# Encoder layer with a 32-expert mixture: TensorE's order by hand from the third expert on, and four bias matmuls at another place

## The chip, the core and the metric

The kernel runs on one core of a Trainium2 chip. The metric is the device time of one execution in microseconds (us). The core's engines run their own instruction lists in order: TensorE (PE; its weight loads are listed apart as PEld), VectorE (DVE), ScalarE (ACT), GpSimd (POOL) and SyncE (SP, which here issues the loads of weights). They wait for each other by semaphores.

## What is computed

One post-norm layer on 1024 tokens of width 1024: attention, a LayerNorm, and then a mixture of experts, in which each token goes to 4 of 32 experts. The part that the change touches is the mixture; cut to it, the reference is:

```python
def clamped_swiglu(h):
    h_glu = jnp.minimum(h[..., 0::2], SWIGLU_LIMIT)
    h_lin = jnp.clip(h[..., 1::2], -SWIGLU_LIMIT, SWIGLU_LIMIT)
    return h_glu * jax.nn.sigmoid(SWIGLU_ALPHA * h_glu) * (h_lin + 1.0)

def expert_block(args):                       # 128 rows of one expert
    xblk, e = args
    h = xblk @ w_gate_up[e] + b_gate_up[e]    # 1024 -> 2048
    return clamped_swiglu(h) @ w_down[e] + b_down[e]   # 1024 -> 1024
```

The result of each block is scaled by the rows' gates and added to the tokens' rows.

## The kernel before

**Experts.** Each expert takes 128 rows; the 18 experts with most tokens (numbers 1 to 6 and then the even ones from 8 to 30; `ovf(e)` is true for them) take 32 rows more, "rows beyond 128". The loop over experts is unrolled, and runs `gate_up(e)` and then `down(e - 1)`, so that an expert's activation is transposed and multiplied by its down weights one expert later.

**Blocks.** `gate_up(e)` runs over 8 blocks k of 128 weight rows (tiles w3g and so on: expert 3, gate and up), `down(e)` over 4 blocks of 256 (w3d). Products of float32 are made in three passes: the weights are split into a rounded part `wh`, by a cast on ACT (L615), and the rest `wl`, by a subtraction on DVE (L620), and the rows into `xTh`, `xTl` (for down: `aTh`, `aTl`). A block is 12 matmuls of 128x512. `wh` and `wl` have three buffers each, so the cast for block k + 3 waits until TensorE has done block k. The matmuls of gate_up add up in PSUM tiles gu_0 and gu_1, those of down in yp, those of the rows beyond 128 in go and yq (groups of 16 matmuls of 32 columns, after the blocks 3 and 7, and at the end of down).

**Biases.** They are matmuls of a one-hot row, `sel`, with the table of biases (tile b3, in the trace b): four into gu at the head of an expert (gu<-b,sel), and four of 32 columns into go (go<-b,sel) for the rows beyond 128.

**Transposes.** The rows reach TensorE transposed. `turn` transposes four pieces of 128x128 into the PSUM tile tp and splits the result: a cast on ACT (L60, `xTh`/`aTh`), then a subtraction on DVE (L61, `xTl`/`aTl`), which is the last reader of tp. **There is one buffer for tp**, so a transposition waits until the one before it has been read out:

```python
            tc.tile_pool(name="moet", bufs=1, space=PSUM, reuse_waits="tile") as ps_t:
...
def turn(src, hi, lo, nk, nm):
    tp = ps_t.tile([P, 4, P], F32, tag="tp", name=f"tp{nm}")
    for c in range(nk):
        nc.tensor.transpose(tp[:, c, :], src[:, c * P:(c + 1) * P], ident)
    ...
        split(hi, lo, tp[:, 0:nk, :])
```

Per expert e these are, in the order in which the code asks for them: tpa_0, tpa_1 and (if expert e - 1 has rows beyond 128) tpao of the activation of e - 1, behind the blocks 0, 1 and 2; and tpx_0, tpx_1 and (if expert e + 1 has such rows) tpxo of the rows of e + 1, behind the blocks 3, 4 and 5 (for e = 2 behind 4, 5 and 6).

**What sets the order.** A scheduler orders each engine's list at compile time by its own estimates of when an instruction can start, and may put a transposition or a bias between two matmuls of a block. Inside `tc.manual_schedule(engines={PE})` TensorE's list keeps the order in which the code is written. Before, this holds for `down` of the experts with rows beyond 128 alone. ACT and DVE are ordered by the scheduler throughout the experts.

Of the kernel before, what the change touches and what calls it, by code (L numbers as in the profile page):

```python
# [20 lines left out]
P = 128  # L21
# [9 lines left out]
OVF = 32  # L31
# [11 lines left out]
def trunk_kernel(ctx: ExitStack, tc: tile.TileContext, x, w_qkv, q_norm, k_norm, w_o,  # L43
# [7 lines left out]
    def mm(o, lhsT, rhs, start=True, stop=True):  # L51
        nc.tensor.matmul(o, lhsT=lhsT, rhs=rhs, start=start, stop=stop)  # L52
# [525 lines left out]
    b3 = keep.tile([P, 2 * D], BF16, name="b3")  # L578
# [4 lines left out]
    sel = keep.tile([P, NE], BF16, name="sel")  # L583
# [461 lines left out]
    with tc.tile_pool(name="moex", bufs=1, side="right", reuse_waits="tile") as mx, \  # L1045
# [83 lines left out]
        def ovf(e):  # L1129
            rank = e if e < 2 else e // 2 + (NE // 2 if e % 2 else 1)  # L1130
            return 1 <= rank <= NO
# [78 lines left out]
        def gate_up(e, between):  # L1210
            gus = [ps_g.tile([P, D], F32, tag=f"gu{h}", name=f"gu{e}_{h}") for h in range(2)]
            gu = [gus[n // 2][:, n % 2 * 512:(n % 2 + 1) * 512] for n in range(4)]
            if ovf(e):
                go = ps_o.tile([P, 512], F32, tag="o", name=f"go{e}")
            for n in range(4):
                sl = slice(n * 512, (n + 1) * 512)
                mm(gu[n], sel[:, e:e + 1].to_broadcast([P, P]), b3[:, sl], True, False)
            for n in range(4 if ovf(e) else 0):
                mm(go[n * OVF:(n + 1) * OVF], sel[:, e:e + 1].to_broadcast([P, OVF]),
                   b3[:, n * 512:(n + 1) * 512], True, False)  # L1220
            act[e], part, whole = swiglu(gus, D, e)
            by_cols = e in (0, NE - 1)
            later = []
            for k in range(KD - 2 if by_cols else KD):
                fetch(ci[0] + len(order))
                prep(ci[0] + 3)
                hi, lo, w = wts.pop((e, "g", k))
                xh, xl = xT[e][0][:, k, :], xT[e][1][:, k, :]
                for n in range(4):
                    sl = slice(n * 512, (n + 1) * 512)  # L1230
                    mm3(gu[n], xh, xl, hi[:, sl], lo[:, sl], False, k == KD - 1)
                later.append((k, w))
                if k % 4 == 4 - 1:
                    for kk, w in later if ovf(e) else ():
                        j, hf = divmod(kk, 2)
                        ts = slice(j * OVF, (j + 1) * OVF)
                        for n in range(4):
                            mm(go[n * OVF:(n + 1) * OVF], xoT[e][:, hf, ts], w[:, n * 512:(n + 1) * 512],
                               False, kk == KD - 1)
                    later.clear()  # L1240
                ci[0] += 1
                if k in between:
                    between[k]()
            if by_cols:

                end = []
                for k in range(KD - 2, KD):
                    fetch(ci[0] + len(order))
                    prep(ci[0] + 3)
                    end.append((k, wts.pop((e, "g", k))))  # L1250
                    ci[0] += 1
                for n in range(4):
                    sl = slice(n * 512, (n + 1) * 512)
                    for k, (hi, lo, w) in end:
                        mm3(gu[n], xT[e][0][:, k, :], xT[e][1][:, k, :], hi[:, sl], lo[:, sl], False, k == KD - 1)
                    if n == 0:
                        for k in (KD - 2, KD - 1):
                            if k in between:
                                between[k]()
                    if n == 1:  # L1260
                        part(0)
                part(1)
            else:
                whole()
            xT.pop(e)
            if ovf(e):
                xoT.pop(e)
                acto[e], _, whole = swiglu([go], 256, f"o{e}")
                whole()

        def down(e, between={}):
            y = ys.pop(e, None) or mp.tile([P, D], F32, tag="y", bufs=2, name=f"y{e}")
            yp = ps_g.tile([P, D], F32, tag="gu0", name=f"yp{e}") if e == NE - 1 else \
                ps_y.tile([P, D], F32, tag="y", name=f"yp{e}")
            if ovf(e):
                yq = ps_o.tile([P, 512], F32, tag="o", name=f"yq{e}")
            ah, al = actT[e]
            later = []
            in_turn = ExitStack()
            if ovf(e):  # L1280
                in_turn.enter_context(tc.manual_schedule(engines={mybir.EngineType.PE}))
            for c in range(KD // 2):
                fetch(ci[0] + len(order))
                prep(ci[0] + 3)
                hi, lo, w = wts.pop((e, "d", c))
                for j in range(2):
                    k = 2 * c + j
                    for n in range(2):
                        sl = slice(j * D + n * 512, j * D + (n + 1) * 512)
                        mm3(yp[:, n * 512:(n + 1) * 512], ah[:, k, :], al[:, k, :], hi[:, sl], lo[:, sl],  # L1290
                            k == 0, k == KD - 1)
                later.append((c, w))
                if c == KD // 2 - 1:
                    for cc, w in later if ovf(e) else ():
                        ts = slice(cc * OVF, (cc + 1) * OVF)
                        for j in range(2):
                            for n in range(2):
                                sl = slice(j * D + n * 512, j * D + (n + 1) * 512)
                                m = 2 * j + n
                                mm(yq[m * OVF:(m + 1) * OVF], actoT[e][:, j, ts], w[:, sl],  # L1300
                                   cc == 0, cc == KD // 2 - 1)
                    later.clear()
                ci[0] += 1
                if c in between:
                    between[c]()
            in_turn.close()
            nc.scalar.mul(y, yp, gm_s[:, e:e + 1])  # L1307
            nc.gpsimd.indirect_dma_start(  # L1308
                out=fd, out_offset=bass.IndirectOffsetOnAxis(ap=mi[:, e:e + 1], axis=0),
                in_=y, in_offset=None, bounds_check=T + P - 1, oob_is_err=True, compute_op=ALU.add)  # L1310
            if not ovf(e):
                return
            H2 = 2 * OVF
            ya = mp.tile([H2, 512], F32, tag="ya", bufs=1, name=f"ya{e}")
            nc.scalar.mul(ya, yq[H2:P], go_s[H2:P, e:e + 1])
            yo = mp.tile([H2, 512], F32, tag="yo", bufs=2, name=f"yo{e}")
            nc.vector.scalar_tensor_tensor(yo, yq[0:H2], go_s[0:H2, e:e + 1], ya, ALU.mult, ALU.add)
            nc.gpsimd.indirect_dma_start(
                out=fd2, out_offset=bass.IndirectOffsetOnAxis(ap=toh[:, e:e + 1], axis=0),
                in_=yo, in_offset=None, bounds_check=2 * (T + P) - 1, oob_is_err=True, compute_op=ALU.add)  # L1320

        fetch(8)
        for e in range(NE):
            between = {}
            if e > 0:
                for part in range(3):
                    between[part] = lambda part=part: turn_a(e - 1, part)
            if e + 1 < NE:
                if e == 0:
                    between[X1] = lambda: [turn_x(1, part) for part in range(3)]  # L1330
                else:
                    for part in range(3):
                        between[(4 if e == 2 else 3) + part] = lambda part=part: turn_x(e + 1, part)
            if e == 0:
                with tc.manual_schedule(engines={mybir.EngineType.DVE}):
                    slots(lambda: prep_lo(2))
            gate_up(e, between)
            if e == 1:
                list_blocks()
            if e + 2 < NE:  # L1340
                gather_x(e + 2)
                gather_o(e + 2)
            if e == NE - 1:
                between = {1 + part: lambda part=part: turn_a(NE - 1, part) for part in range(3)}
                down(e - 1, between)
            elif e > 0:
                down(e - 1)
        down(NE - 1)

    es_w.close()  # L1350

# [141 lines left out]
```

## Time and profile before

| | |
|---|---|
| time, median of 3 runs | 2091.97 us (2090.58 to 2093.69) |
| the profiled execution: own time, span | 2091.31 us, 2089.5 us |
| TensorE (PE) busy | 1999.2 us, 96% of the span |
| DVE, ACT busy | 1636.2 us (78%), 1284.1 us (61%) |
| mean granted TensorE clock | 0.984 of full speed |

The span is the time from the first to the last instruction; 1.8 us of the execution lie around it. Busy is the sum of the durations of an engine's instructions. Matmuls are pipelined and their records overlap, so TensorE's pace is read from the starts of neighbouring rows, and not from their durations. The clock is given as a share of 2.4 GHz: 1.00 is full speed, 0.50 the level of 1.2 GHz.

### The profile page before, as it was taken

Reading aid. Unit: us, or ns where it says so; the run is one execution under the profiler, and the core shown is the slowest. Engines: PE = TensorE matmul, PEld = TensorE weight load, DVE = VectorE, ACT = ScalarE, POOL = GpSimd, SP = SyncE. Lnnn points to the kernel's source line nnn. Section 1 sums busy time; section 2 is a strip of 40 time slices with the busy share of each in tenths; the row PEclk is TensorE's granted clock in tenths of the full one; section 3 lists DMA queues with packets and bytes.
Section 4 is the critical chain, followed back from the end, with each engine's and each line's share of the span. In section 5 each row is a group of like instructions: output and inputs, shape, how many; then the busy total and the mean of one; then the engine's idle time right before and its main releaser. Section 6 shows DMA issues by size and latency. Waiting matters only on the chain. (4 is left out here: it accounts for less than half of the span.)

```text
span 2089.5 us, 27609 instructions
## 1 busy us (share of the span) xinstructions
PE 1999.2 (96%) x10059; PEld 1358.2 (65%) x10091; DVE 1636.2 (78%) x1771; ACT 1284.1 (61%) x1548; POOL 555.2 (27%) x382
## 2 busy tenths in 40 slices
PE   8999999999997999999999999999999999999990
PEld 6774444444675666666776776777767767777670
DVE  5658778887887877777887887878878878788786
ACT  5656655565554656656676766766767667667662
POOL 0216676766134311110210102111111021110114
PEclk9999999999998999999999999999999999999995
DMA  5216000000545778788897897898978978989764
GB/s 173 71 61 177 31 31 21 31 21 11 205 148 205 278 283 301 272 302 287 328 376 293 333 349 294 346 343 307 377 290 334 349 297 345 339 302 379 267 248 174
DMA packets 106348, 500.36 MB, mean 239 GB/s; under 512 B 16001, under 2 KB 17026, under 8 KB 73442
## 3 DMA queue, kind: packets, MB, share of 16 engines
q1 hardware_dynamic: 86928, 445.45, 55.3%
q0 software_dynamic: 16432, 52.47, 9.1%
q8 instruction: 80, 1.31, 0.3%
q10 hardware_dynamic: 2850, 0.66, 0.1%
q14 instruction: 58, 0.48, 0.1%
HBM read 457.05 MB, written 41.49 MB: 239 GB/s over the span
## 5 line engine op out<-in xcount | busy, mean ns | idle before, releaser
L52 PE MATMUL gu<-wh,xTh 128*128 128x512 f32 x1024 | 415.3, 406 | 1.0 <-ACT xTh L60 1.0
L52 PE MATMUL gu<-wh,xTl 128*128 128x512 f32 x1024 | 410.5, 401 | 0.0
L52 PE MATMUL gu<-wl,xTh 128*128 128x512 f32 x1024 | 401.9, 393 | 0.0
L1308 POOL DMA_INDIRECT fd<-y,mi x32 | 78.8, 2464 | 660.5 <-ACT y L1307 656.8
L447 ACT ACTIVATE pt<-st 128x512 f32<-128x512 f32 x256 | 150.6, 597 | 134.8 <-PE st L52 110.1
L52 PEld LDWEIGHTS gu<-wh,xTh 128*128 128x128 f32 x1024 | 193.4, 189 | 42.3 <-ACT xTh L60 1.7
L52 PEld LDWEIGHTS gu<-wh,xTl 128*128 128x128 f32 x1024 | 193.9, 189 | 38.5 <-issue 3.6
L52 PEld LDWEIGHTS gu<-wl,xTh 128*128 128x128 f32 x1024 | 193.3, 189 | 39.4 <-issue 0.2
L451 POOL TENSOR_TENSOR acc<-acc,pt 128x512 f32<-128x512 f32 x152 | 201.2, 1324 | 48.8 <-ACT pt L447 39.8
L52 PE MATMUL yp<-wl,aTh 128*128 128x512 f32 x512 | 204.5, 399 | 0.4 <-DVE wl L620 0.4
L52 PE MATMUL yp<-wh,aTh 128*128 128x512 f32 x512 | 201.8, 394 | 0.0
L52 PE MATMUL yp<-wh,aTl 128*128 128x512 f32 x512 | 200.0, 391 | 0.0
L437 DVE TENSOR_REDUCE nm<-sc 128x1 f32<-128x1024 f32 x124 | 150.5, 1221 | 29.1 <-PE sc L52 28.1
L52 PE MATMUL po<-pt,vn 128*64 128x512 f32 x512 | 135.7, 616 | 2.1 <-DVE ot L472 2.1
L606 POOL DMA_INDIRECT xg<-xd,mi x32 | 54.6, 1706 | 291.6 <-PE tpx L1145 282.5
L52 PE MATMUL qkv<-wh,xT 128*128 128x512 f32 x384 | 124.2, 404 | 2.6 <-ACT xT L60 1.4
L52 PE MATMUL st<-qs,kT_hi 128*128 128x512 f32 x256 | 116.7, 456 | 3.4 <-ACT pt L447 3.2
L52 PEld LDWEIGHTS yp<-wh,aTh 128*128 128x128 f32 x512 | 96.2, 188 | 33.5 <-ACT act L1189 14.2
L52 PEld LDWEIGHTS st<-qs,kT_hi 128*128 128x128 f32 x256 | 48.0, 188 | 97.7 <-ACT pt L447 66.7
L52 PEld LDWEIGHTS yp<-wl,aTh 128*128 128x128 f32 x512 | 96.4, 188 | 21.8 <-DVE wl L620 1.2
L52 PEld LDWEIGHTS yp<-wh,aTl 128*128 128x128 f32 x512 | 96.2, 188 | 20.2 <-issue 0.8
L52 PE MATMUL st<-q,kT_lo 128*128 128x512 f32 x256 | 102.4, 400 | 0.6 <-DVE q L155 0.6
(515 smaller groups left out, 4179.4 us busy)
## 6 DMA issues: line engine op xcount, KB each, us to landing
w0g<-in_expert_w_gate_up SPq DMA_DIRECT2D x8, 1024.0 KB, 19.6
w1g<-in_expert_w_gate_up SPq DMA_DIRECT2D x8, 1024.0 KB, 7.8
w2g<-in_expert_w_gate_up SPq DMA_DIRECT2D x8, 1024.0 KB, 10.4
w3g<-in_expert_w_gate_up SPq DMA_DIRECT2D x8, 1024.0 KB, 8.5
w4g<-in_expert_w_gate_up SPq DMA_DIRECT2D x8, 1024.0 KB, 6.4
w5g<-in_expert_w_gate_up SPq DMA_DIRECT2D x8, 1024.0 KB, 6.4
w6g<-in_expert_w_gate_up SPq DMA_DIRECT2D x8, 1024.0 KB, 6.5
w7g<-in_expert_w_gate_up SPq DMA_DIRECT2D x8, 1024.0 KB, 7.1
```

Source lines behind the costliest of these rows:

```text
L52: nc.tensor.matmul(o, lhsT=lhsT, rhs=rhs, start=start, stop=stop)
L437: nc.vector.tensor_reduce(nms[n][:, m:m + 1], sc.pop((n, m)), AX.X, ALU.max, negate=True)
L447: nc.scalar.activation(pts[n, k], st, AF.Exp)
L451: (nc.vector if k == 7 or n == NG - 1 or n == NG - 2 and k > 3 else nc.gpsimd).tensor_tensor(accs[n], pts[n, 0] if k == 1 else accs[n], pt ...
L606: return nc.gpsimd.indirect_dma_start(out=xg[e], out_offset=None, in_=xd, in_offset=bass.IndirectOffsetOnAxis(ap=mi[:, e:e + 1] if rows is ...
L1308: nc.gpsimd.indirect_dma_start(out=fd, out_offset=bass.IndirectOffsetOnAxis(ap=mi[:, e:e + 1], axis=0), in_=y, in_offset=None, bounds_chec ...
```

## The change

The context for TensorE's own order is opened once, after `gate_up(1)` and `list_blocks()`, and closed after the last `down`, in place of one context for each `down` of an expert with rows beyond 128. So from expert 2 (the third) on TensorE's list is the order of the code. In `gate_up`, the four bias matmuls into go move from the head of the expert to just ahead of the first group of matmuls into go, behind block 3.

```diff
@@ gate_up
             for n in range(4):
                 sl = slice(n * 512, (n + 1) * 512)
                 mm(gu[n], sel[:, e:e + 1].to_broadcast([P, P]), b3[:, sl], True, False)
-            for n in range(4 if ovf(e) else 0):
-                mm(go[n * OVF:(n + 1) * OVF], sel[:, e:e + 1].to_broadcast([P, OVF]),
-                   b3[:, n * 512:(n + 1) * 512], True, False)
...
                 if k % 4 == 4 - 1:
+                    for n in range(4 if ovf(e) and k == 4 - 1 else 0):
+                        mm(go[n * OVF:(n + 1) * OVF], sel[:, e:e + 1].to_broadcast([P, OVF]),
+                           b3[:, n * 512:(n + 1) * 512], True, False)
                     for kk, w in later if ovf(e) else ():
@@ down
-            in_turn = ExitStack()
-            if ovf(e):
-                in_turn.enter_context(tc.manual_schedule(engines={mybir.EngineType.PE}))
...
-            in_turn.close()
@@ the loop over experts
         fetch(8)
+        in_turn = ExitStack()
         for e in range(NE):
...
             gate_up(e, between)
             if e == 1:
                 list_blocks()
+
+                in_turn.enter_context(tc.manual_schedule(engines={mybir.EngineType.PE}))
...
         down(NE - 1)
+        in_turn.close()
```

What this does to the lists: no instruction is added or taken away on TensorE. On it 30 tpa_1, 18 tpao, 13 tpx_1 and 16 tpxo stand earlier, the 68 matmuls go<-b,sel of 17 experts later, and in 12 experts the gu<-b,sel later; near the very end a few matmuls change places.

TensorE, expert 13, from the end of block 1 on (the tile wh_10648 is block 2's; tpa_1 is the second transposition of expert 12's activation). Before:

```order
L52 MATMUL gu_1_10639<-wh_10618,xTl_10437 128x512
L52 MATMUL gu_1_10639<-wl_10620,xTh_10436 128x512
L52 MATMUL gu_0_10638<-wh_10648,xTh_10436 128x512
L52 MATMUL gu_0_10638<-wh_10648,xTl_10437 128x512
L52 MATMUL gu_0_10638<-wl_10650,xTh_10436 128x512
L52 MATMUL gu_0_10638<-wh_10648,xTh_10436 128x512
L52 MATMUL gu_0_10638<-wh_10648,xTl_10437 128x512
L52 MATMUL gu_0_10638<-wl_10650,xTh_10436 128x512
L52 MATMUL gu_1_10639<-wh_10648,xTh_10436 128x512
L1145 MATMUL tpa_1_10692<-ident,act_10320 128x128 x4
L52 MATMUL gu_1_10639<-wh_10648,xTl_10437 128x512
```

And with the change (wh_10626 is block 2's):

```order
L52 MATMUL gu_1_10617<-wh_10596,xTh_10414 128x512
L52 MATMUL gu_1_10617<-wh_10596,xTl_10415 128x512
L52 MATMUL gu_1_10617<-wl_10598,xTh_10414 128x512
L1145 MATMUL tpa_1_10670<-ident,act_10294 128x128 x4
L52 MATMUL gu_0_10616<-wh_10626,xTh_10414 128x512
L52 MATMUL gu_0_10616<-wh_10626,xTl_10415 128x512
L52 MATMUL gu_0_10616<-wl_10628,xTh_10414 128x512
```

tpa_1 stood behind seven matmuls of block 2 and now stands ahead of all of them. Between tpa_0 and tpa_1 there were 19 matmuls and there are 12.

TensorE, expert 14, at the biases of its rows beyond 128. Before they stood inside block 0:

```order
L52 MATMUL gu_1_10958<-wh_10895,xTh_10749 128x512
L52 LDWEIGHTS sel
L52 MATMUL go_10959<-b_4716,sel 32x512
L52 LDWEIGHTS sel
L52 MATMUL go_10959<-b_4716,sel 32x512
L52 LDWEIGHTS sel
L52 MATMUL go_10959<-b_4716,sel 32x512
L52 LDWEIGHTS sel
L52 MATMUL go_10959<-b_4716,sel 32x512
L52 MATMUL gu_1_10958<-wh_10895,xTl_10750 128x512
```

With the change they stand behind the last matmul of block 3:

```order
L52 MATMUL gu_1_10933<-wl_10972,xTh_10727 128x512
L52 LDWEIGHTS sel
L52 MATMUL go_10934<-b_4716,sel 32x512
L52 LDWEIGHTS sel
L52 MATMUL go_10934<-b_4716,sel 32x512
L52 LDWEIGHTS sel
L52 MATMUL go_10934<-b_4716,sel 32x512
L52 LDWEIGHTS sel
L52 MATMUL go_10934<-b_4716,sel 32x512
L52 MATMUL go_10934<-w14g_10709,xoT_10729 32x512 x4
```

They moved next to the other matmuls into go.

ScalarE, expert 2, at the store of the list of further blocks (bt) and its load into blk, which waits until the store has landed. Before:

```order
L615 CAST wh_6973<-w2g_6797 128x2048
L1147 COPY aoT_6906<-tpao_6957 128x256
L615 CAST wh_7007<-w2g_6815 128x2048
L1125 DMA bt<-ebi 128x2
L615 CAST wh_7035<-w2g_6833 128x2048
L1127 DMA blk<-bt 1x256
L60 CAST xTh_7023<-tpx_0_7026 128x512
```

With the change:

```order
L615 CAST wh_6971<-w2g_6799 128x2048
L1147 COPY aoT_6904<-tpao_6955 128x256
L1125 DMA bt<-ebi 128x2
L615 CAST wh_7009<-w2g_6817 128x2048
L1127 DMA blk<-bt 1x256
L615 CAST wh_7037<-w2g_6835 128x2048
L60 CAST xTh_7025<-tpx_0_7028 128x512
```

The store is issued one cast earlier. Apart from this place and the last expert, ACT and DVE keep their order; in particular DVE still has the subtraction for the weights of block 3 (L620) right ahead of the one that reads out tpa_0 (L61).

## Rows read from the trace of the kernel before

**Rows 1.** Who waited for whom, TensorE, 930 to 2060 us: total, times, longest.

```profile
PE yp L52 <- DVE wl L620: 0.4, 1, 0.4
```

**Rows 2.** Timeline of TensorE, expert 13: start, duration, instruction, count.

```profile
1238.49 0.60 PE L1145 MATMUL tpa<-ident,act 128*128 128x128 f32 x4
...
1241.69 0.39 PE L52 MATMUL gu<-wh,xTh 128*128 128x512 f32 x1
...
1243.06 0.39 PE L52 MATMUL gu<-wh,xTh 128*128 128x512 f32 x1
1243.34 0.66 PE L1145 MATMUL tpa<-ident,act 128*128 128x128 f32 x4
...
1246.60 0.39 PE L1145 MATMUL tpao<-ident,acto 128*128 128x128 f32 x2
```

**Rows 3.** Timeline of ScalarE, the same stretch.

```profile
1238.45 1.91 ACT L615 CAST wh<-w13g 128x2048 fp32r<-128x2048 f32 x1 [0.73 <-PE gu L52]
1240.27 0.58 ACT L60 CAST aTh<-tpa 128x512 fp32r<-128x512 f32 x1
```

**Rows 4.** Timeline of VectorE, the same stretch.

```profile
1240.39 2.29 DVE L620 TENSOR_TENSOR wl<-w13g,wh 128x2048 fp32r<-128x2048 f32 x1 [1.36 <-ACT wh L615]
1242.60 0.68 DVE L61 TENSOR_TENSOR aTl<-tpa,aTh 128x512 fp32r<-128x512 f32 x1
```

**Rows 5.** Timeline of TensorE, expert 12: a pair of transposes with 12 matmuls between.

```profile
1208.26 0.66 PE L1145 MATMUL tpx<-ident,xg 128*128 128x128 f32 x4
...
1211.51 0.60 PE L1145 MATMUL tpx<-ident,xg 128*128 128x128 f32 x4
```

**Rows 6.** Timeline of TensorE, expert 31: the last pair with 19 matmuls between.

```profile
1991.57 0.60 PE L1145 MATMUL tpa<-ident,act 128*128 128x128 f32 x4
...
1996.43 0.66 PE L1145 MATMUL tpa<-ident,act 128*128 128x128 f32 x4
```

**Rows 7.** Timeline of TensorE, expert 2.

```profile
767.78 0.81 PE L1145 MATMUL tpx<-ident,xg 128*128 128x128 f32 x4 [2.56 <-DVE xTl L61]
768.25 0.78 PE L52 MATMUL gu<-wh,xTl 128*128 128x512 f32 x1
...
771.71 0.40 PE L52 MATMUL gu<-wh,xTh 128*128 128x512 f32 x1
```

**Rows 8.** Windows: busy us (count) of PE, PEld, DVE, ACT, POOL; granted clock; DMA; GB/s.

```profile
160.00:172.00 12.00, 8.41 (x34) 5.08 (x33) 10.77 (x21) 8.03 (x25) 5.15 (x8) 1.00 0.37 92
765.00:770.00 5.00, 2.44 (x9) 1.93 (x9) 1.86 (x2) 2.87 (x3) 1.06 (x1) 0.82 0.51 148
```

**Rows 9.** Timeline of TensorE, expert 14: matmuls ahead of and behind its go<-b,sel.

```profile
1277.12 0.39 PE L52 MATMUL gu<-wh,xTh 128*128 128x512 f32 x1
...
1278.34 0.40 PE L52 MATMUL gu<-wh,xTh 128*128 128x512 f32 x1
```

**Rows 10.** Timeline of TensorE, head of expert 2: go<-b,sel behind another bias.

```profile
740.88 0.40 PE L52 MATMUL go<-b,sel 128*32 128x512 bf16 x4
741.21 0.50 PE L52 MATMUL gu<-wh,xTh 128*128 128x512 f32 x1
```

**Rows 11.** Timeline of TensorE, down of expert 6, with expert 8's gu<-b,sel.

```profile
1017.84 0.39 PE L52 MATMUL yp<-wh,aTl 128*128 128x512 f32 x1
...
1018.74 0.40 PE L52 MATMUL yp<-wh,aTh 128*128 128x512 f32 x1
...
1020.89 3.64 PE L52 MATMUL yq<-w6d,aoT 128*32 128x512 f32 x32
...
1024.92 0.40 PE L52 MATMUL gu<-wh,xTl 128*128 128x512 f32 x1
```

**Rows 12.** Timeline of TensorE, head of expert 3: all four gu<-b,sel behind yq.

```profile
788.78 3.64 PE L52 MATMUL yq<-w1d,aoT 128*32 128x512 f32 x32
...
793.46 0.39 PE L52 MATMUL gu<-wh,xTl 128*128 128x512 f32 x1
```

**Rows 13.** Timeline of TensorE in the attention stage.

```profile
163.83 0.27 PE L154 MATMUL tpm<-ident,nm 128*8 128x128 f32 x1 [1.56 <-DVE nm L147]
```

## Prediction

> **What bounds the kernel now.** I read first who waits for whom. From 930 us to the end of the experts one wait of TensorE for another engine is listed, of 0.4 us [rows 1]: TensorE is the bound there, and every matmul that leaves a place where it covered something costs its full time. So I then looked, in the timelines of TensorE, ScalarE and VectorE, at what the moved instructions wait for.
>
> The transposes are the ones that wait. All share one PSUM tile, tp, and its last reader is DVE's subtraction L61. In expert 13, tpa_0 starts at 1238.49 and tpa_1 at 1243.34 [rows 2], 4.85 us later. What fills this time stands on the other two engines. Block 0's end frees a buffer; ACT casts the weights of block 3 from 1238.45 for 1.91 us, and only then aTh out of tp, at 1240.27 [rows 3]. DVE subtracts those weights from 1240.39 for 2.29 us, and then reads out tp from 1242.60 to 1243.28 [rows 4]. tpa_1 starts 0.06 us after that. So the scheduler has put tpa_1 almost exactly where tp comes free, and the seven matmuls of block 2 ahead of it, whose first and last start at 1241.69 and 1243.06 (0.228 us from one to the next) [rows 2], cover the wait. That is why no wait for a transposition is listed.
>
> **The change part by part.**
>
> *Transposes at the block's end.* Now tpa_1 stands ahead of those seven matmuls. ACT and DVE keep their order, and their chain starts from the end of block 0, which doesn't move against tpa_0; so tpa_1 still can't start before 4.85 us. TensorE comes to it earlier: a transposition and 12 matmuls take 1211.51 - 1208.26 = 3.25 us, measured where nothing is waited for [rows 5]. It keeps its order, so it stands still for 4.85 - 3.25 = **1.60 us**, with seven ready matmuls queued behind the transposition, and runs them afterwards (7 x 0.228 = 1.60). Nothing gives this back, since TensorE is the bound.
>
> What is late next? tpao comes 12 matmuls after tpa_1 in both orders; before, it started 3.26 us after it [rows 2], which is what the 12 matmuls take. Its chain on ACT and DVE hangs on the end of block 1, which comes before the stall, so tpao meets it as before. The casts of later blocks shift with TensorE. tpx_0 starts a new chain from block 3, and a tpx_1 that stood 19 matmuls behind it stalls the same way.
>
> How many: of the moved transposes, 29 tpa_1 (experts 3 to 31), 12 tpx_1 (odd experts 7 to 29) and 3 tpxo (experts 3 to 5) stood 19 matmuls and 4.85 or 4.86 us behind the transposition ahead (the last pair: 1996.43 - 1991.57 [rows 6]), and now stand 12 behind. The other moved tpao and tpxo keep 12 matmuls to the one ahead. In even experts the group of matmuls into go stands between block 3 and tpx_0 and gives ACT and DVE the time; tpx_1 there stood at 3.25 us already [rows 5] and stays. So 44 x 1.60 = **+70.4 us**.
>
> *Expert 2* is counted apart. Its tpx_1 already waits 2.56 us [rows 7], because on ACT the cast of tpx_0 stands behind the load of blk, and that behind the landing of the store bt. The next 8 matmuls take 771.71 - 768.25 = 3.46 us instead of 8 x 0.228 = 1.82 [rows 7], 1.64 us more, in a window with a granted clock of 0.82 [rows 8]. With the change the store is issued one cast earlier, so most of this should go, while tpa_1 and tpx_1 get stalls of the new kind. I set the sum at 0, with bounds of -4.2 (2.56 + 1.64 gone, no new stall) and +3.2 (two stalls on top).
>
> *go<-b,sel.* Inside block 0 of expert 14 they cost 1278.34 - 1277.12 = 1.22 us less the 0.68 of the three matmuls in it: 0.54 [rows 9]. The new place is not in the trace; in the nearest row they follow another bias, and it is 0.33 us up to the next matmul [rows 10]. Bounds for the cost: nothing and 0.54. I take 0.33, since here too instructions of another kind stand ahead and four small loads come one behind another. Saved: 0.21 x 17 = **-3.6 us**; bounds 0 and -9.2.
>
> *gu<-b,sel* of 12 even experts. Two of the four cost 0.90 us less two matmuls, 0.44, inside yp; the first, ahead of these, is put at the same 0.22; the fourth stood behind yq, with 4.03 us from yq to the second matmul into gu [rows 11]. With all four behind yq, as at expert 3, this takes 4.68 us [rows 12]: 0.65 more against 0.66 saved, so **0**; bounds 0 and -7.9 (12 x 0.66).
>
> *Last expert:* a few matmuls change places within blocks; left out.
>
> Sum: 70.4 - 3.6 = +66.8 us. On the profiled execution's 2091.31 us that is 2158.1; its time lies 0.7 us under the median of the runs, 2091.97, so **2159 us**, 3.2% slower. With all bounds added up this case reaches from +49 (70.4 - 9.2 - 7.9 - 4.2) to +74 (70.4 + 3.2), 2141 to 2166 us.
>
> **The rivals.**
>
> *Not slower: tp is free by the block's end.* If DVE had read out tpa_0 within 3.25 us, the moves would cost nothing and the biases would save 3.6 us: 2088 us, and 2075 with the bounds of the biases. For it: no wait for a transposition is listed before [rows 1], and 4.85 us could be just the 19 matmuls. Against it: DVE's row ends at 1243.28 [rows 4], 1.6 us after block 2 begins [rows 2], and everything ahead of it on ACT and DVE is ordered as before. It decides if the L61 row comes 1.6 us earlier against tpa_0; if it came half as early, 2092 + 35 - 4 = 2123 us.
>
> *The clock falls at the stalls.* After the idle 2.56 us at 767.78 matmuls started 0.43 us apart, the pace of the 1.2 GHz level, which cost 1.64 us [rows 7, 8]. If each of the 44 stalls did this, 72 us come on top: 2231 us; with a third of them, 2183. Against it: TensorE idled 1.56 us ahead of 163.83 [rows 13], and 160 to 172 us, where it was busy for 8.41 of 12 us, shows a granted clock of 1.00 [rows 8]; a stall of 1.60 us is nearer to that row. The Trainium skill, page "TensorE: Matmul & The Clock Gate", section "A second HAM failure mode: psum-queue depth-cycling", speaks against this change: a TensorE that idles a little between groups of matmuls while it cycles through PSUM has its clock swing between its two levels and loses throughput. By that rule the time would be the 2231 us; of the trace, the row at 767.78 agrees with it and the window at 160 us does not.
>
> *Stalls in a row.* If a stall also made the following chain late, tpao and tpxo behind it would wait too: 18 + 12 of them, 30 x 1.6 = 48 us more, 2207 us. Against it: the chain behind tpa_1 starts at the end of block 1, ahead of the stall.
>
> **How the numbers follow.** Forecast 0.80; tp free early 0.08 (0.05 of it fully, 0.03 so that other losses cancel it); clock 0.08; stalls in a row 0.04. The range goes from 2140, the lower bound of the forecast's own case, to 2184, which takes in a clock that falls at a third of the stalls. A measurement of this kernel tells about 0.2% (4 us) from no change. Faster by more than that 0.05, within it 0.03, slower 0.92.
>
> **What would show it.** After the change TensorE's waits should list tpa and tpx behind DVE's L61, over 40 times at about 1.6 us, some 70 us in all; from tpa_0 to tpa_1 still 4.85 us, now with 12 matmuls; from tpa_1 to tpao 3.25 us without a wait; go<-b,sel 0.33 us ahead of the group into go; a granted clock of 1.00 through the experts; in expert 2 a shorter wait at tpx_1. I am wrong if the L61 row comes well under 4.8 us after tpa_0, if matmuls start 0.43 us apart behind the stalls, or if tpao and tpxo get waits of their own.

## The result, and the profile after

| | before | after |
|---|---|---|
| median of the runs, us | 2091.39 (6 runs, 2090.58 to 2093.69) | 2162.92 (6 runs, 2161.41 to 2165.95) |
| ratio to before, 95% interval | 1 | 1.0341 (1.0331 to 1.0351) |
| profiled execution: span, us | 2089.5 | 2161.7 |
| TensorE busy, us | 1999.2 (96%) | 2002.9 (93%) |

The change makes the kernel 71.5 us slower, where +66.8 was forecast. TensorE's busy time hardly grew: the loss is idle time. The view of who waits for whom, TensorE of the kernel after, 790 to 2130 us, answers to [rows 1] (total, times, longest):

```profile
PE tpa L1145 <- DVE aTl L61: 43.2, 29, 1.5
PE tpx L1145 <- DVE xTl L61: 18.0, 12, 1.5
PE tpxo L1145 <- DVE xTl L61: 4.5, 3, 1.5
PE yp L52 <- DVE wl L620: 4.2, 13, 0.4
PE gu L52 <- DVE wl L620: 0.3, 1, 0.3
```

The first three lines are the 44 stalls, 29 + 12 + 3, with 65.7 us of idle time. The fourth was not forecast; one of its 13 waits stood there before too [rows 1]. The timeline of TensorE in expert 13, against [rows 2]:

```profile
1264.20 0.60 PE L1145 MATMUL tpa<-ident,act 128*128 128x128 f32 x4
...
1267.18 0.39 PE L52 MATMUL gu<-wl,xTh 128*128 128x512 f32 x1
1269.06 0.66 PE L1145 MATMUL tpa<-ident,act 128*128 128x128 f32 x4 [1.49 <-DVE aTl L61]
...
1272.32 0.39 PE L1145 MATMUL tpao<-ident,acto 128*128 128x128 f32 x2
```

From tpa_0 to tpa_1 it is 1269.06 - 1264.20 = 4.86 us, as before, now with 12 matmuls in place of 19. The last of these starts at 1267.18 and ends 0.39 us later; then TensorE stands still for 1.49 us by the record, 1.60 us by the starts (4.86 - 3.25). tpao follows 3.26 us behind tpa_1, without a wait. ScalarE in the same stretch, against [rows 3]:

```profile
1264.17 1.91 ACT L615 CAST wh<-w13g 128x2048 fp32r<-128x2048 f32 x1 [0.72 <-PE gu L52]
1265.98 0.58 ACT L60 CAST aTh<-tpa 128x512 fp32r<-128x512 f32 x1
```

VectorE, against [rows 4]:

```profile
1266.11 2.29 DVE L620 TENSOR_TENSOR wl<-w13g,wh 128x2048 fp32r<-128x2048 f32 x1 [1.35 <-ACT wh L615]
1268.32 0.68 DVE L61 TENSOR_TENSOR aTl<-tpa,aTh 128x512 fp32r<-128x512 f32 x1
```

The chain is the one of before, to 0.1 us: cast 1.91, subtraction 2.29, read-out 0.68; tpa_1 starts 0.06 us after the read-out. The experts' window (busy us of PE, PEld, DVE, ACT, POOL; granted clock; DMA; GB/s) shows no fall of the clock:

```profile
790.00:2115.00 1325.00, 1252.14 (x6532) 890.43 (x6524) 1000.25 (x680) 817.90 (x593) 164.31 (x88) 1.00 0.80 301
```

For the wait that was not forecast, the timeline of TensorE through down of expert 12: the first matmul, those around the wait, the start of yq, and the second matmul of expert 14 behind it. Before:

```profile
1260.22 0.39 PE L52 MATMUL yp<-wh,aTh 128*128 128x512 f32 x1
...
1268.88 0.39 PE L52 MATMUL yp<-wh,aTl 128*128 128x512 f32 x1
1269.34 0.38 PE L52 MATMUL gu<-b,sel 128*128 128x512 bf16 x1
1269.37 0.58 PE L52 MATMUL yp<-wl,aTh 128*128 128x512 f32 x1
1269.78 0.40 PE L52 MATMUL yp<-wh,aTh 128*128 128x512 f32 x1
...
1271.92 3.64 PE L52 MATMUL yq<-w12d,aoT 128*32 128x512 f32 x32
...
1275.96 0.40 PE L52 MATMUL gu<-wh,xTl 128*128 128x512 f32 x1
```

After:

```profile
1289.13 0.39 PE L52 MATMUL yp<-wh,aTh 128*128 128x512 f32 x1
...
1297.54 0.39 PE L52 MATMUL yp<-wh,aTl 128*128 128x512 f32 x1
1298.25 0.50 PE L52 MATMUL yp<-wl,aTh 128*128 128x512 f32 x1 [0.32 <-DVE wl L620]
1298.59 0.40 PE L52 MATMUL yp<-wh,aTh 128*128 128x512 f32 x1
...
1300.78 3.64 PE L52 MATMUL yq<-w12d,aoT 128*32 128x512 f32 x32
...
1305.47 0.40 PE L52 MATMUL gu<-wh,xTl 128*128 128x512 f32 x1
```

VectorE, the subtraction that makes the last wl of this down, before and after:

```profile
1267.00 2.29 DVE L620 TENSOR_TENSOR wl<-w12d,wh 128x2048 fp32r<-128x2048 f32 x1
```

```profile
1295.91 2.28 DVE L620 TENSOR_TENSOR wl<-w12d,wh 128x2048 fp32r<-128x2048 f32 x1
```

15.74 us have become 16.34. Before, one bias stood behind the 26th matmul of down and two behind the 38th, right ahead of the 39th, the first that reads this wl. (The trace shows one of the two: the profile before has 10059 matmul records for 10091 weight loads.) With the biases TensorE was busy until wl was there, at 1267.00 + 2.29 = 1269.29. Now nothing stands there: TensorE could start the 39th matmul at 1297.54 + 0.23 = 1297.77, wl is there at 1295.91 + 2.28 = 1298.19, and TensorE waits. From 1297.54 to 1298.59 two matmuls take 1.05 us in place of 2 x 0.228: the wait costs 0.59 us in all.

### The profile page after: what moved, and what is told of

It reads as the page before. It is cut to its first block, busy times and chain, and to the rows that moved or that the text cites. A ratio compares the mean times of both kernels' runs of the same rounds, so it can differ in the third digit from the quotient of the medians.

```text
span 2161.7 us, 27640 instructions
## 1 busy us (share of the span) xinstructions
PE 2002.9 (93%) x10091; PEld 1357.1 (63%) x10091; DVE 1635.6 (76%) x1771; ACT 1280.5 (59%) x1548; POOL 525.2 (24%) x382
## 5 line engine op out<-in xcount | busy, mean ns | idle before, releaser
L52 PE MATMUL gu<-wh,xTh 128*128 128x512 f32 x1024 | 422.0, 412 | 0.8 <-ACT xTh L60 0.8
L52 PE MATMUL gu<-wh,xTl 128*128 128x512 f32 x1024 | 400.9, 392 | 0.0
```

## The experiments

The theory: the loss is the distance of 44 transposes from the one ahead, on the one buffer tp. The rivals: the moved biases cause it, the clock, or a hand order that costs in some other way.

**1. The 44 places undone, all else kept.** Per block, the transposition is called behind the seventh matmul of the next block:

```diff
-                    mm3(gu[n], xh, xl, hi[:, sl], lo[:, sl], False, k == KD - 1)
+                    mm(gu[n], xh, hi[:, sl], False, False)
+                    if n == 2 and (k, 7) in between:
+                        between[k, 7]()
+                    mm(gu[n], xl, hi[:, sl], False, False)
+                    mm(gu[n], xh, lo[:, sl], False, k == KD - 1)
...
-                    between[part] = lambda part=part: turn_a(e - 1, part)
+                    between[(part + 1, 7) if part and e > 2 else part] = lambda part=part: turn_a(e - 1, part)
...
-                        between[(4 if e == 2 else 3) + part] = lambda part=part: turn_x(e + 1, part)
+                        k = (4 if e == 2 else 3) + part
+                        late = e > 2 and (part == 2 or part == 1 and not ovf(e))
+                        between[(k + 1, 7) if late else k] = lambda part=part: turn_x(e + 1, part)
```

> The changed kernel with only the 44 stalled transposes and those that follow them (tpa_1, tpao, tpxo, and tpx_1 of experts without rows beyond 128, from expert 3 on) written seven matmuls into the next block, where the scheduler had them. All else is as in the changed kernel, the hand order and the biases included; expert 2 is as there. Theory: no waits for L61 outside expert 2, 2162.9 - 44 x 1.60 = 2092.5 us (2088 to 2096). Rival (the order by hand costs by something else than these places, as the waits of yp for wl or the grouped gu<-b,sel): well above 2096 us.

Measured 2092.16 us, 1.0003 (0.9994 to 1.0012) of before. Its waits of TensorE from 735 us on, the first three rows:

```profile
PE yp L52 <- DVE wl L620: 4.1, 13, 0.4
PE tpa L1145 <- DVE aTl L61: 2.1, 1, 2.1
PE tpx L1145 <- DVE xTl L61: 1.5, 1, 1.5
```

The two that are left for L61 are expert 2's. The places of 44 transposes cost 2162.92 - 2092.16 = 70.8 us, 1.61 us each.

**2. Three matmuls in place of seven.** The same edit with 3 for 7.

> As the version with the transposes seven matmuls into the next block, but only three matmuls in, with the same lists on ScalarE and VectorE. Theory (a transposition starts when tp has been read out, 4.85 us after the one ahead, and each matmul written ahead of it covers 0.228 us): 44 stalls of 1.60 - 3 x 0.228 = 0.92 us remain, 2092.2 + 44 x 0.92 = 2132.5 us, and the list of waits shows about 36 to 40 us for L61 from expert 3 on. Rival (some fixed cost of a transposition at the block's end, such as a changed pattern of weight loads or the clock, and not its distance): either about 2163 or about 2092 us.

Measured 2132.73 us, 1.0200 (1.0184 to 1.0216). Its waits from 790 us on:

```profile
PE tpa L1145 <- DVE aTl L61: 23.4, 29, 0.8
PE tpx L1145 <- DVE xTl L61: 9.9, 12, 0.8
...
PE tpxo L1145 <- DVE xTl L61: 2.4, 3, 0.8
```

The loss goes with the number of matmuls that cover the wait, 0.92 us for each stall, as the theory has it; nothing fixed is lost by a transposition at a block's end.

**3. Still 12 matmuls apart, but with a shorter chain.** The transposes stand five matmuls ahead of their block's end, so that ScalarE's and VectorE's lists have the read-out ahead of the next weights (`mm3` is taken apart as in experiment 1):

```diff
-                    between[part] = lambda part=part: turn_a(e - 1, part)
+                    between[(part, 7) if e > 2 else part] = lambda part=part: turn_a(e - 1, part)
...
-                        between[(4 if e == 2 else 3) + part] = lambda part=part: turn_x(e + 1, part)
+                        k = (4 if e == 2 else 3) + part
+                        between[(k, 7) if e > 2 else k] = lambda part=part: turn_x(e + 1, part)
```

> The changed kernel with every transposition from expert 3 on written five matmuls ahead of its block's end; they are 12 matmuls apart, as in the changed kernel, and on ScalarE and VectorE the scheduler now puts the read-out of tp ahead of the cast and the subtraction of the weights (but for tpao and tpx_0 in some places, where one subtraction stands ahead). Theory (not the distance of 12 matmuls costs, but the chain that starts with a cast of 1.91 us and a subtraction of 2.29 us): the read-out takes about 2 us from the transposition, under the 3.25 us, and the stalls are gone: 2092.5 us, as for the late places (2088 to 2100). Rival 1 (12 matmuls are too near whatever the order): the time stays above 2140 us. Rival 2 (the subtractions of the weights become late behind the read-outs, since 2.29 + 0.68 us is more than a block's 2.75 us): waits of TensorE for wl, about 1 us in each expert, some 2120 us.

Measured 2092.94 us, 1.0002 (0.9993 to 1.0011); no wait for L61 from expert 3 on, and none for wl but those of the version above. In expert 13 TensorE shows

```profile
1240.74 0.60 PE L1145 MATMUL tpa<-ident,act 128*128 128x128 f32 x4
1243.95 0.60 PE L1145 MATMUL tpa<-ident,act 128*128 128x128 f32 x4
```

and ScalarE

```profile
1241.37 0.59 ACT L60 CAST aTh<-tpa 128x512 fp32r<-128x512 f32 x1 [0.24 <-PE tpa L1145]
1242.31 1.91 ACT L615 CAST wh<-w13g 128x2048 fp32r<-128x2048 f32 x1 [0.35 <-PE gu L52]
```

and VectorE

```profile
1242.36 0.68 DVE L61 TENSOR_TENSOR aTl<-tpa,aTh 128x512 fp32r<-128x512 f32 x1
```

So tp has been read out at 1243.04, 2.3 us after tpa_0 and under the 3.2 us of 12 matmuls. It isn't the distance by itself but the cast and the subtraction that stood ahead of the read-out.

**4. The moved go<-b,sel alone.** The kernel before with only the second part of the diff.

> The kernel before with the move of go<-b,sel alone; the transposes keep the places that the scheduler gave them. Theory (44 stalls behind the one tp buffer make the whole loss): no transposition is listed as waiting, and the time falls by 17 times what a group of four saves. The profile after shows that a group costs 0.19 us at the new place (9.83 us from tpa_1 to tpx_0 in expert 14, against 8.05 + 7 x 0.227 without it) where 0.54 us was read at the old one: 17 x 0.35 = 6 us less, about 2085.5 us (2087.8 by the prediction's 0.21). Rival (the moved biases cost something themselves, or disturb the first group into go): 2095 us or more.

Measured 2086.51 us, 0.9973 (0.9963 to 0.9983) against 2092.06: 5.6 us less, 0.33 for each of 17 groups. The moved biases help; that rival falls.

**5. The order by hand alone.** The changed kernel with go<-b,sel back at the head of the expert.

> The changed kernel with go<-b,sel back at the head of the expert; the order by hand stays. Theory: the same 44 stalls, about 66 us of waits for L61 in TensorE's list; the biases cost 0.33 us at the head in place of 0.19, 17 x 0.14 = 2.4 us more than the changed kernel, about 2165 us (2163 to 2169). Rival (the moved biases bring the stalls or their time): under 2140 us.

Measured 2177.98 us, 1.0412 (1.0397 to 1.0426): 15.1 us over the changed kernel in place of 2.4. The stalls are the same, 65.5 us. What the theory had missed is a wait of its own, in the view of waits and at expert 14 on TensorE:

```profile
PE go L52 <- DVE yo L1313: 9.8, 16, 0.6
```

```profile
1313.06 0.40 PE L52 MATMUL go<-b,sel 128*32 128x512 bf16 x4 [0.61 <-DVE yo L1313]
```

go and yq share one PSUM buffer (tag "o"). At the head of the expert yq has only just been finished, and its last reader on VectorE, yo, starts at 1312.27 and takes 0.74 us. Behind block 3 yq is long read out: in the changed kernel yo ends at 1305.95 and go<-b,sel starts at 1318.92. This wait and the dearer place of experiment 4 make up the 15.1 us: 9.8 + 17 x 0.33 = 15.4. The two parts of the change depend on each other: in this hand-written order the biases cost 15.1 us more at the head of the expert than behind block 3.

**6. The wait for wl covered by other work.** The first half of the matmuls into yq goes ahead of block 2 of down, in the version of experiment 1:

```diff
-                if c == KD // 2 - 1:
+                if c % 2 == 1:
                     for cc, w in later if ovf(e) else ():
```

> The version with the transposes seven matmuls into the next block, and in down of the experts with rows beyond 128 the first half of the matmuls into yq moved from the end of down to behind block 1, ahead of the matmul of block 2 that waits for VectorE's wl. Nothing is added, and gu<-b,sel stay grouped behind yq. Theory (the 5 us that the hand order loses beside the stalls is TensorE's wait for wl in down, once in 13 experts, which the biases had covered before): the wait goes, and with it 13 x 0.37 = 4.8 us: 2087.4 us (2086 to 2089). Rival (the group of four gu<-b,sel behind yq costs it by itself): 2092 us or a little more.

Measured 2094.03 us, 1.0014 (1.0005 to 1.0023); the waits of yp are gone but for one, and the time isn't better. Where there had been no such wait (experts 1 to 5) down takes 16.18 us in place of 15.78: a second group costs 0.40 us. In the other 12 it takes 16.05 in place of 16.30, so the wait was worth 0.25 + 0.40 = 0.65 us, and 12 x 0.25 - 5 x 0.40 leaves 1.0 us to gain, less than the medians tell apart. (The matmul that waits is the 39th, in block 3 counted from 0, and not in block 2 as the expectation has it; the cover, 14 matmuls ahead of it, makes TensorE late enough all the same.) The wait is real, and the cover costs nearly as much; this run alone can't name the biases.

**7. Three of the four gu<-b,sel back in down.** In the version of experiment 1, for 12 even experts:

```diff
+                at = {26: [0], 38: [1, 2]}
...
+                            done += 1
+                            for q in at.get(done, ()):
+                                bias(gu, f, q)
```

> The version with the transposes seven matmuls into the next block, and in 12 even experts three of the four gu<-b,sel written where the scheduler had them, behind the 26th and the 38th matmul of down. Together this is the scheduler's list with the moved go<-b,sel, written by hand, but for four transposes of expert 2 and two matmuls of the last expert. Theory (what the order by hand costs is the places of the 44 transposes and of these biases, and nothing else): 2086.5 us, as measured for the scheduler's list with the moved biases, within 2 us; the waits of yp for wl are gone. Rival (a loss of another kind): 2090 us or more.

Measured 2087.46 us, 0.9976 (0.9966 to 0.9986), 4.7 us under experiment 1 and level with experiment 4, whose list it nearly is. In its profile down of these experts takes 15.74 us again. Written by hand in these places, the order costs nothing that the runs show: what costs is where the hand put 44 transposes and the biases of 12 experts.

**8 and 9. Longer stalls, for the clock.** tpa_1 stands five, or two, matmuls ahead of block 1's end (five is shown; for two the place is `(1, 10)`):

```diff
-                    between[part] = lambda part=part: turn_a(e - 1, part)
+                    between[(1, 7) if part == 1 and e > 2 else part] = lambda part=part: turn_a(e - 1, part)
```

> The changed kernel with tpa_1 of the experts from the third on written five matmuls earlier, seven behind tpa_0, to lengthen 29 stalls from 1.60 to 1.60 + 5 x 0.228 = 2.74 us, longer than the 2.56 us after which the kernel before showed the half clock in expert 2. The read-out of tpa_1 moves ahead of one cast and one subtraction. Theory (a stall costs its own time alone): 2162.9 + 29 x 1.14 = 2196 us, granted clock near 1.00. Rival (a stall of this length brings the clock down, at some 1.6 us each as at expert 2): 2196 + 29 x 1.6 = 2242 us, with matmuls 0.43 us apart behind tpa_1.

> As the version with tpa_1 five matmuls earlier, but two matmuls earlier: 29 stalls of 1.60 + 2 x 0.228 = 2.06 us, listed as about 1.95. With five matmuls 20 of 29 stalls (listed as 2.63 us) were followed by matmuls at half pace, at 1.60 us each; with none, 0 of 44 (listed as 1.49 us). Without any fall of the clock: 2162.9 + 29 x 0.46 = 2176.2 us. If all 29 bring the clock down: 2176.2 + 46 = 2222 us. Theory (a stall of this length, like that of 2.08 us in expert 2 of the changed kernel, brings it down in part of the cases): between, near 2200 us, 1.6 us for each that does.

Measured 2226.01 us (1.0642, 1.0626 to 1.0659) and 2185.04 us (1.0446, 1.0430 to 1.0462), both between the two cases. Two stalls of the first, on TensorE, each with the tpao that follows 17 matmuls later:

```profile
959.62 0.66 PE L1145 MATMUL tpa<-ident,act 128*128 128x128 f32 x4 [2.63 <-DVE aTl L61]
...
964.00 0.38 PE L1145 MATMUL tpao<-ident,acto 128*128 128x128 f32 x2
...
1291.54 0.66 PE L1145 MATMUL tpa<-ident,act 128*128 128x128 f32 x4 [2.63 <-DVE aTl L61]
...
1293.49 0.63 PE L52 MATMUL gu<-wh,xTh 128*128 128x512 f32 x1
1293.92 0.63 PE L52 MATMUL gu<-wh,xTl 128*128 128x512 f32 x1
...
1297.54 0.38 PE L1145 MATMUL tpao<-ident,acto 128*128 128x128 f32 x2
```

Windows behind the two stalls (busy us of PE, PEld, DVE, ACT, POOL; granted clock; DMA; GB/s):

```profile
959.60:964.00 4.40, 4.38 (x21) 3.64 (x22) 1.51 (x2) 2.53 (x3) 1.03 (x1) 1.00 0.98 357
1294.00:1296.00 2.00, 2.00 (x6) 1.57 (x5) 0.77 (x1) 1.20 (x1) 0.00 (x0) 0.50 1.02 268
```

The first pair takes 4.38 us, with a granted clock of 1.00; the second takes 6.00, with matmuls 0.43 us apart and a granted clock of 0.50, the 1.2 GHz level. In the profiled execution such a stretch followed 20 of 29 stalls of 2.63 us, at 1.6 us each: 2196 + 20 x 1.6 = 2228. It followed 8 of 29 stalls of 1.93 us (2176.2 + 8 x 1.6 = 2189, the profiled execution's own time; the median lies 4 us lower), and none of the 44 of 1.49 us in the changed kernel.

**10. The hand-written list, with expert 2's transposes also seven matmuls later.**

> The hand-written version of the scheduler's list (transposes seven matmuls into the next block, three of the gu<-b,sel inside down, go<-b,sel at the head of their group), with the transposes of expert 2 seven matmuls later as well. Theory: in expert 2 the stalls of 2.08 and 1.53 us go, but for about 0.5 us, and with them the stretch at half clock that costs 1.6 us: 2087.5 - 4.7 = 2082.8 us (2081 to 2085), faster than both kernels. Rival (the store and load of the list of blocks on ScalarE bring the wait of 2.4 us at tpx_1 back): about 2086 us.

Measured 2086.75 us, 0.9976 (0.9967 to 0.9985). The rival came true: in expert 2 the waits of TensorE are

```profile
PE tpx L1145 <- DVE xTl L61: 2.7, 1, 2.7
PE tpa L1145 <- DVE aTl L61: 0.5, 1, 0.5
```

and on ScalarE the read-out of tpx_0 is again behind the load of blk, which waits for the landing of the store bt:

```profile
768.16 0.59 ACT L60 CAST xTh<-tpx 128x512 fp32r<-128x512 f32 x1 [4.40 <-DMA bt<-ebi]
```

It is 0.24% faster than the kernel before and 76 us faster than the changed one, like experiments 4 and 7, from which it can't be told apart; the simplest of the three is experiment 4, the move of four biases in the kernel before.

## Why the prediction was right, and what it missed

- **Transposes at the block's end**, +70.4: right in mechanism, count and size. 44 stalls, 70.8 us by experiment 1, and the dose of experiment 2 came within 0.3 us. tpao and tpx behind a stall had no wait of their own, so "Stalls in a row" falls; "Not slower: tp is free by the block's end" falls with the waits listed, and experiment 3 shows what it would have taken: a read-out ahead of the cast.
- **"The clock falls at the stalls"**: falls for this change, with a granted clock of 1.00 and 0 of 44, but less safely than argued. The row that spoke against it (1.56 us, [rows 13]) was the right one to lean on; stalls of 1.93 us already bring the clock down in 8 of 29 cases. The Trainium skill, page "TensorE: Matmul & The Clock Gate", section "A second HAM failure mode: psum-queue depth-cycling", has TensorE's clock swing, in a bf16 kernel that cycles through PSUM, when it idles a little between groups of matmuls: at 1.49 us the runs don't show it, at 1.93 and 2.63 us they do.
- **go<-b,sel**, -3.6: right in sign, too small; -5.6 by the medians of experiment 4, -5.3 by its profile with expert 2 left out. The mis-sized term is the cost at the new place: 0.33 us was taken from a bias behind another bias at an expert's head, 0.19 is what a group costs there (the reading ahead of experiment 4: 9.83 - 8.05 - 7 x 0.227). Why it is cheaper right ahead of other matmuls into go, no run shows.
- **gu<-b,sel of 12 even experts**, 0: the step that failed. Of "0.65 more against 0.66 saved" the first holds: from yq to the second matmul into gu it is now 1305.47 - 1300.78 = 4.69 us, where it was 4.04 in expert 12. The second doesn't, because the prediction did not ask what the three biases ahead of yq covered. With them TensorE came to the 39th matmul when its wl was there; without them it comes 0.42 us too early and the wait costs 0.59 us, so that 0.07 of the 0.66 is saved. In the profiles this makes 12 x 0.55 = 6.6 us from experiment 7 to experiment 1; their medians lie 4.7 us apart. It was in sight in the trace before: without the two biases the 39th matmul would have come at 1268.88 + 0.23 = 1269.11, and without the first one 0.23 us earlier still, while VectorE has its wl ready at 1269.29.
- **Expert 2**, 0: right within what can be measured. The wait of 2.56 us at tpx_1 went and stalls of 2.1 and 1.5 us came, the first of them followed by matmuls at half pace in this profile (4.83 us from tpa_1 to tpao in place of 3.25); from expert 2's first transposition to expert 3's it is 53.04 us after and 52.45 before.

The medians give 70.8 - 5.6 + 4.7 = 69.9 us, where 71.5 was measured. They scatter: the time up to expert 1's first transposition, in which TensorE's lists are the same in all these kernels, takes 700.4 us in one profile and 705.9 in another. The stage behind it can be read by itself. From expert 3's first transposition to the end of the last matmul into yp the profiles have:

| kernel | us |
|---|---|
| before | 1243.36 |
| after | 1315.27 |
| experiment 1 | 1245.39 |
| experiment 4 | 1238.61 |
| experiment 7 | 1238.77 |

So the places of the transposes cost 1315.27 - 1245.39 = 69.9 us, 16 of the 17 groups of go<-b,sel save 1243.36 - 1238.61 = 4.8, and gu<-b,sel cost 1245.39 - 1238.77 = 6.6: together +71.7, and the stage became 71.9 us longer. That the forecast of +66.8 lies within 5 us of the result is in part luck: it gave the biases into go too little and those into gu nothing, and these two misses have opposite signs.

## What to carry to other kernels

Before an instruction is moved in the list of the engine that is the bound, ask two things of its old place: what it waits for, and what the instructions around it cover. A place that looks arbitrary, seven matmuls into a block, can be the moment at which a single buffer comes free, and a small filler between two matmuls can hide a wait that no view lists. Where a wait on a single buffer can't be covered, shorten what stands ahead of its last reader on the other engines instead; experiment 3 did, and was level with the kernel before. And to price such a move, compare the length of the stage that it touches between profiles, and not the whole time alone.

## What was not expected of the hardware

The fall of TensorE's clock is not decided by the length of the stall ahead of it alone. In one execution each, stalls of the same listed length, 2.63 us, at the same place of their experts, were followed by 1.2 GHz in 20 of 29 cases, and of 1.93 us in 8 of 29; a fall lasted 4 to 8 matmuls and cost 1.3 to 1.6 us. In expert 2 a stall of 2.08 us brought the clock down in the changed kernel and not in experiment 1, and one of 2.38 us in experiment 4 did not either: from 770 to 775 us, right behind it, the granted clock is 1.00. The eight falls behind 1.93 us came in the experts 7, 11, 15, 19, 20, 21, 25 and 29, nearly every fourth. What decides in the single case stays open.
